# The feed-forward of a hybrid decoder layer in two phases, with seven half products for the first product too

## The chip, the cores and the metric

The kernel runs on one core of one Trainium2 chip. A core has five engines with queues of their own: TensorE (in profiles PE, its weight loads PEld), VectorE (DVE), ScalarE (ACT), GpSimd (POOL) and SyncE (SP), and 16 DMA engines that all queues share. SBUF is the working memory of 128 partitions, PSUM holds the matmul sums in banks of 512 fp32 columns. The metric is the time of one execution on the device, in microseconds (us). Given are the median of the runs and one execution recorded by the hardware profiler.

## The reference

One decoder layer for one sequence of 512 tokens, model width 2048, all in float32:

- `mod = silu(c) @ w_ada + b_ada` gives six vectors of 2048 (shift, scale and gate of the mixer, then of the feed-forward).
- `h = rmsnorm(x) * (1 + scale) + shift`, `proj = h @ w_in`, then eight HGRN2 heads and eight gated-delta heads of width 128, `y = concat(heads) @ w_out` and `x = x + gate * rmsnorm(y)`.
- The feed-forward (FF):

```python
h = rmsnorm(x, pre_ffn_norm[l]) * (1.0 + sc_f) + sh_f
y = jnp.square(jax.nn.relu(h @ w_ff1[l])) @ w_ff2[l]
x = x + gt_f * rmsnorm(y, post_ffn_norm[l])
```

`w_ff1` is 2048 x 8192, `w_ff2` 8192 x 2048. Both FF products have the same number of multiplications.

## The kernel before

**Three matmuls for one.** Every float32 matrix product is split: an operand is rounded to a high part H (`copy` into the type fp32r) and the rest is the low part L (a subtraction). `mm3` (its matmuls are recorded under line 296) multiplies H by H, H by L and L by H into one PSUM bank. So each weight piece needs a cast on ScalarE (L165) and a subtraction on VectorE (L167, for a few early pieces on GpSimd) beside its load.

**The weight stream.** `WeightStream` holds a plan of all weight pieces in the order of use. A piece is 128 partitions x 1024 floats, 512 KB. `get` hands out the split halves of the next piece and, ahead of that, issues loads on SP's queue and splits a few pieces on. SP's queue works in order: a load that waits for its buffer holds up those behind it.

**The layer's stages.** The start computes the modulation and the first projections; then the heads run while TensorE works through the remaining projections; then the output product (`pout`), in four column blocks; then the residual, the norm and 64 transposes (`pm`) that give `h2H` and `h2L`, the transposed FF input; then the FF; then norm, gate, residual and store. In the FF the order of TensorE's and SP's instructions is that of the program; the other engines' is laid out by a planner by its own costs.

**The FF before.** The 8192 inner columns are cut into 16 row blocks `r` of 512 (`RB` = 4 columns of 128). `ff1(r, g)` computes half a block (`pf`): 4 pieces, each 24 matmuls of 512 tokens; ScalarE takes Relu and Square into `g` (L1544, L1545). The second product uses Winograd's form of Strassen's scheme: both operands are cut into quarters, and seven products of sums of quarters replace eight products. `combos(r)` forms and splits the sums of activations (L1555 to L1567), `ff2s(r, m)` the seven products for half the output columns, 12 matmuls of 512 columns for each piece (`px`, `pg`). The sums of weight quarters are formed by DMAs that add to a loaded buffer, issued by GpSimd (L142, `chain`, `raw`). After each product VectorE adds the PSUM bank to the output `y2` in SBUF (L1607, L1609). The order is `ff1` of block r+1 and `ff2s` of block r in turn:

```python
for r in range(NR - 1):
    last = r == NR - 2
    yield from ((1, r + 1, 0), (2, r, 0))
    yield from ((2, r, 1), (1, r + 1, 1)) if last else ((1, r + 1, 1), (2, r, 1))
```

The last block's second product is done plainly (`plan_f2`, `ff2`). During the FF `ada_gtf` also works off the last part of `w_ada`, the FF gate: 64 loads of 256 KB, for each a product on ScalarE (L414) and a sum on GpSimd (L416), one step for every fourth weight piece; the eight `pgf` matmuls and the gate's weighting follow in the tail.

Of the kernel before, what the change touches and what calls it, by code (L numbers as in the profile page):

```python
# [8 lines left out]
F32 = mybir.dt.float32  # L9
# [48 lines left out]
ADA_REST = (4, 3, 2, 5)  # L58


def by_tiles(name, a):
# [26 lines left out]
    if name == "w_ff1":  # L88
        return a[0].reshape(4, 4, P, DFF // 256, 256).transpose(3, 0, 2, 1, 4).reshape(-1, P, 1024)
# [4 lines left out]

class WeightStream:


# [10 lines left out]
    def start(self):  # L108

        self.loads, self.upto = [], []  # L110
        for i, e in enumerate(self.plan):
            two = e[0][0] == "s2"
            if e[1] is not None:
                self.loads.append((i, e[1], e[2] if two else None))
            self.upto.append(len(self.loads))
        self.nraw = self.nw = 0
        self.wide = None

    def _raw(self, chain):
        if chain:  # L120
            return self.wide.tile([P, 1024], F32, tag="chain", name=f"chain{self.nl}", bufs=2)
        i = self.nraw
        self.nraw += 1
        pool, tag, nb = self.pool, "raw", self.bufs[0]
        if self.wide is not None and i % 2:
            pool, tag = self.wide, "raw2"
        return pool.tile([P, 1024], F32, tag=tag, name=f"raw{i}", bufs=nb)

    def _load(self):
        key, ap, kind = self.loads[self.nl]  # L130
        raw = self._raw(kind is not None and kind[0])
        self.nc.sync.dma_start(out=raw, in_=ap[0])
        if kind is not None and kind[1] is not None:
            self._add(raw, kind[1])
# [5 lines left out]
    def _add(self, raw, ap):  # L140

        self.nc.gpsimd.dma_start(out=raw, in_=ap[0], accum_op=ALU.add)  # L142

    def _split(self):
        i = self.ns
        e = self.plan[i]
        pool, nb = self.pool, self.bufs
        two = e[0][0] == "s2"
        raw = self.raw.pop(i)
        hn = ln = None  # L150
        if not two and len(e) > 2:
# [5 lines left out]
        if hn is None:  # L157
            tags = ("wh", "wl")
            if self.wide is not None and (two or len(e) == 2):
# [8 lines left out]
        if two and e[3] is not None:  # L168
            self._add(raw, e[3][1])
            self.raw[i + e[3][0]] = raw  # L170
        k = 2 if two else e[1][1]
# [4 lines left out]
        self.ns += 1  # L176

    def get(self, key):
# [3 lines left out]
        sa = self.sa if self.wide is None else 2  # L182
        su = min(n, i + 1 + max(2, sa))
        st = min(n, i + 1 + sa)
# [1600 lines left out]
```

## Time and profile before

| | |
|---|---|
| median of 3 runs | 2586.01 us (2584.15 to 2588.4) |
| the profiled execution's own time | 2584.08 us |
| its span, first to last instruction | 2582.4 us |
| mean granted TensorE clock | 0.985 |
| first FF matmul, last of the seven-product FF | 1247 us, 2501 us |
| read from HBM, written | 418.65 MB, 8.40 MB |

A row of a group reads: line, engine, operation, output <- inputs by the program's names, shape, count, then busy time in us, mean ns of one, and idle time of the engine before it with what ended it. A row of a stretch reads: start:end, length, busy time of PE, PEld, DVE, ACT and POOL with counts, granted clock, share of the DMA engines, GB/s. A row of the timeline reads: start, length, engine, line, operation. Matmuls are pipelined: the length of one is its latency, and the distance between two starts is what it costs.

### The profile page before, as it was taken

How to read it: one execution, taken by the hardware profiler on the slowest of the kernel's cores; microseconds unless marked ns; L12 is line 12 of the kernel's file. 1: busy time of each engine (PE TensorE's matmuls, PEld its weight loads, DVE VectorE, ACT ScalarE, POOL GpSimd, SP SyncE). 2: the span in 40 equal slices, each digit the busy share in tenths (PEclk: the TensorE clock that was granted, in tenths of full speed). 3: DMA queues.
4: the chain of work that ended last, by engine and by line, in shares of the span. 5: the costliest groups of instructions: out<-in, count | busy, mean ns of one | idle time of the engine just before them, and what ended most of it. 6: DMA issues, size and time to landing. Idle time of an engine off the chain costs nothing.

```text
span 2582.4 us, 34387 instructions
## 1 busy us (share of the span) xinstructions
PE 2470.5 (96%) x12627; PEld 2007.1 (78%) x12627; DVE 1733.7 (67%) x2697; ACT 1121.9 (43%) x1795; POOL 695.1 (27%) x616
## 2 busy tenths in 40 slices
PE   5889999998999899999999999999999999999998
PEld 3667777777777778788788888888888888888886
DVE  7997887768586765634657575665656666575676
ACT  5454544544444442433534444444444444444333
POOL 5561244445445440000112112212121111100003
PEclk9899999999999999999999999999999999999999
DMA  8762334444444432344466666766667666665663
GB/s 315 254 203 77 129 121 142 140 152 137 159 146 158 142 117 82 125 145 152 173 166 178 182 197 168 207 176 179 176 194 199 179 182 177 189 178 149 185 165 155
DMA packets 148903, 429.32 MB, mean 166 GB/s; under 512 B 16647, under 2 KB 21113, under 8 KB 147581
## 3 DMA queue, kind: packets, MB, share of 16 engines
q1 hardware_dynamic: 131258, 364.14, 40.5%
q0 software_dynamic: 17280, 62.92, 14.1%
q8 instruction: 99, 1.62, 0.3%
q14 instruction: 70, 0.57, 0.1%
q10 hardware_dynamic: 196, 0.06, 0.0%
HBM read 418.65 MB, written 8.40 MB: 165 GB/s over the span
## 4 chain that ended last, share of the span: by engine, by line
PE 68%; DVE 4%; POOL 1%; ACT 1%; issue 1%; DMA 1%; DVEq 0%; SPq 0%; ACTq 0%; POOLq 0%
PE pf L296 27%; PE px L296 13%; PE pg L296 10%; PE pj L296 9%; PE pout L296 7%; DVE wl L167 1%; PE pa L296 1%; DMA ada<-in_w_ada_dram 1%; POOL y L1709 0%; DVE uc L999 0%; POOL aacc L416 0%; DVE utmp L997 0%; DVE x2r L1727 0%; PE p L296 0%; DVE zkT L458 0%
## 5 line engine op out<-in xcount | busy, mean ns | idle before, releaser
L165 ACT CAST wh<-raw 128x1024 fp32r<-128x1024 f32 x422 | 443.7, 1052 | 779.8 <-PE pf L296 229.5
L167 DVE TENSOR_TENSOR wl<-raw,wh 128x1024 fp32r<-128x1024 f32 x416 | 529.2, 1276 | 365.9 <-ACT wh L165 361.8
L296 PE MATMUL pf<-h2L,wh 128*128 128x512 f32 x1024 | 399.4, 390 | 0.0
L296 PE MATMUL pf<-h2H,wh 128*128 128x512 f32 x1024 | 399.3, 390 | 0.0
L296 PE MATMUL pf<-h2H,wl 128*128 128x512 f32 x1024 | 399.1, 390 | 0.0
L416 POOL TENSOR_TENSOR aacc<-ada,aacc 128x512 f32<-128x512 f32 x180 | 268.9, 1494 | 253.5 <-ACT ada L414 242.2
L296 PE MATMUL pj<-hH,wh 128*128 128x512 f32 x768 | 324.8, 423 | 0.0
L296 PE MATMUL pj<-hH,wl 128*128 128x512 f32 x768 | 304.7, 397 | 4.4 <-DVE wl L167 4.4
L296 PE MATMUL pj<-hL,wh 128*128 128x512 f32 x768 | 303.6, 395 | 0.0
L296 PEld LDWEIGHTS pf<-h2H,wh 128*128 128x128 f32 x1024 | 192.6, 188 | 39.8
L296 PEld LDWEIGHTS pf<-h2L,wh 128*128 128x128 f32 x1024 | 192.5, 188 | 39.8
L296 PEld LDWEIGHTS pf<-h2H,wl 128*128 128x128 f32 x1024 | 192.5, 188 | 39.7
L142 POOL DMA_DIRECT2D chain<-in_w_ff_dram x90 | 79.0, 877 | 535.4 <-DVE wl L167 316.6
L167 DVE TENSOR_TENSOR wl<-chain,wh 128x1024 fp32r<-128x1024 f32 x90 | 110.9, 1233 | 160.1 <-ACT wh L165 160.1
L296 PE MATMUL px<-wh,cH 128*128 128x512 f32 x480 | 186.9, 389 | 0.4 <-DVE y L1607 0.4
L296 PE MATMUL px<-wh,cL 128*128 128x512 f32 x480 | 186.7, 389 | 0.0
L296 PE MATMUL px<-wl,cH 128*128 128x512 f32 x480 | 186.7, 389 | 0.0
L165 ACT CAST wh<-chain 128x1024 fp32r<-128x1024 f32 x90 | 94.9, 1054 | 201.9 <-PE pf L296 98.3
L296 PEld LDWEIGHTS pj<-hH,wl 128*128 128x128 f32 x768 | 146.3, 190 | 39.5 <-DVE wl L167 6.5
L296 PEld LDWEIGHTS pj<-hH,wh 128*128 128x128 f32 x768 | 146.7, 191 | 28.9
L414 ACT ACTIVATE ada<-ada,c 128x512 f32<-128x512 f32 x244 | 166.2, 716 | 0.0
L296 PEld LDWEIGHTS pj<-hL,wh 128*128 128x128 f32 x768 | 146.9, 191 | 23.4
(450 smaller groups left out, 4493.1 us busy)
## 6 DMA issues: line engine op xcount, KB each, us to landing
raw<-in_w_ff_dram SPq DMA_DIRECT2D x256, 512.0 KB, 5.0
raw<-in_w_in_dram SPq DMA_DIRECT2D x128, 512.0 KB, 3.3
ada<-in_w_ada_dram SPq DMA_DIRECT2D x256, 256.0 KB, 3.0
chain<-in_w_ff_dram POOLq DMA_DIRECT2D x90, 512.0 KB, 5.6
adas<-in_w_ada_dram SPq DMA_DIRECT2D x128, 256.0 KB, 4.3
raw<-in_w_out_dram SPq DMA_DIRECT2D x40, 512.0 KB, 3.5
chain<-in_w_ff_dram SPq DMA_DIRECT2D x30, 512.0 KB, 5.2
raw<-in_w_ff_dram POOLq DMA_DIRECT2D x30, 512.0 KB, 5.4
```

Source lines behind the costliest of these rows:

```text
L142: self.nc.gpsimd.dma_start(out=raw, in_=ap[0], accum_op=ALU.add)
L165: self.cast = self.nc.scalar.copy(out=h, in_=raw).ins
L167: eng.tensor_tensor(out=lo, in0=raw, in1=h.bitcast(F32), op=ALU.subtract)
L296: nc.tensor.matmul(ps, lhsT=lhsT, rhs=rhs, start=start, stop=stop, skip_group_check=chain)
L414: nc.scalar.activation(out=dst[:, s], in_=a[:, s], func=AF.Copy, scale=c2[:, r0 + r : r0 + r + 1])
L416: nc.gpsimd.tensor_tensor(out=acc, in0=a, in1=acc, op=ALU.add)
```

## The change

The FF is done in two phases: all first products, then all second products.

- **Phase 1.** Row block 0 is computed plainly (`ff1_plain`, 192 matmuls of 512 tokens). For blocks 1 to 15 `ff1` computes seven products: the tokens are cut into two halves of 256, the inner width of 2048 and the block's columns in two each, so each product has 2 column groups x 8 x 3 matmuls of 256 tokens. `h_sums` forms and splits the sums of `h` once; the quarter sums of the weights are formed as the second product's are. ScalarE copies partial PSUM sums out, VectorE adds them, then Relu and Square follow. `g_sums` forms the sums of the activations and `spill` writes seven 256 KB tiles of a block to DRAM.
- **Phase 2.** `ff2s(c, m)` takes two row blocks at once (the first chunk one), so a PSUM bank collects both before VectorE adds it to `y2`. `combos` reads the activation sums back from DRAM and splits them. The order of the products is 1, 2, 5, 6, 3, 7, 4; products 1, 6, 7, 4 go on in one bank, 5 and 3 in another.
- **Weight sums.** `steps_of` plans each sum of quarters: two by accumulating DMA, one on GpSimd, one on VectorE in phase 1 (`WAYS1`); two by DMA, two on GpSimd in phase 2 (`WAYS2`). Raw buffers are 3 + 7 instead of 3 + 3 and 2 for the chains, and a load is issued as soon as its buffer is free by the program's count.
- **The FF gate.** `ada_gtf` moves into the output product, three steps for each weight piece; its `pgf` matmuls come before the last two `pre_norm`s, and the finished row goes to DRAM (`gfd`) and is read back in the tail.
- In the norm before the FF the values of `h` are kept in fp32 (`hs`) for the sums; each transposed tile takes an activation and a cast on ScalarE and one subtraction.

```diff
+WAYS1 = ("dma", "pool", "dve", "dma")
+WAYS2 = ("dma", "pool", "pool", "dma")
...
+ORDER = (1, 2, 5, 6, 3, 7, 4)
+def steps_of(key, n, k, quarter, ways):
+    out = []
+    for i in ORDER:
+        for t in range(n):
+            c, d, e = ((key, q, t) for q in ("11", "22", "12"))
+            src = lambda j, q: quarter(q, t) if ways[j] == "dma" else (key, q, t)
+            loads, raw, then = {
+                1: ([(c, "11")], c, [(0, c, "12")]),
+                2: ([((key, "21", t), "21")], (key, "21", t), []),
+                5: ([(d, "22")], c, [(1, c, "22")]),
+                6: ([(e, "12")], c, [(3, c, "21"), (2, e, "22")]),
+                3: ([], d, []),
+                7: ([], e, []),
+                4: ([], c, []),
+            }[i]
...
+    PATTERN = "2212212212"
...
+        if step:
+            for how, out, src in e[4]:
+                self.uses[out] -= 1
+                o = self.raw[out]
+                if how == "dma":
+                    self.nc.gpsimd.dma_start(out=o, in_=src, accum_op=ALU.add)
+                else:
+                    self.uses[src] -= 1
+                    eng = self.nc.gpsimd if how == "pool" else self.nc.vector
+                    eng.tensor_tensor(out=o, in0=o, in1=self.raw[src], op=ALU.add)
...
+    CHUNKS = [(0,)] + [(r, r + 1) for r in range(1, NR - 1, 2)]
+    for r in range(1, NR):
+        plan += steps_of(("f1", r), 2, 8, f1_quarter(r), WAYS1)
+    for c_, rs in enumerate(CHUNKS):
+        for m in range(2):
+            plan += steps_of(("s2", c_, m), len(rs), 2, f2_quarter(rs, m), WAYS2)
...
-    ws = WeightStream(nc, wpool, plan, 3, 1, (3, 2, 2))
+    ws = WeightStream(nc, wpool, plan, 3, 1, (3, 2, 2, 7))
...
+        def on_get():
+            for _ in range(3):
+                next(gsteps, None)
...
+        def ff1(r, A):
+            G = gslots(r)
+            xs = [xbank(f"px{r}_{u}") for u in range(2)]
+            ys, es = [None] * 2, [stage(f"e{r}_{u}", (P, 4, 256)) for u in range(2)]
+            for i in ORDER:
+                for u in range(2):
+                    wH, wL = ws.get(("f1", r, i, u))
...
+                    for k in range(8):
+                        mm3(ps, wH[:, k, :], wL[:, k, :], A[i][0][:, k, :], A[i][1][:, k, :],
+                            k == 0 and i in (1, 2, 5), k == 7 and i in (2, 3, 4), i != 2)
+                    e = es[u]
+                    if i in (1, 5, 6):
+                        nc.scalar.copy(out=e[:, (1, 5, 6).index(i), :], in_=ps)
+                    elif i == 4:
+                        nc.scalar.activation(out=G[:, 0, u, :], in_=ps, func=AF.Relu)
+                    else:
...
+                        nc.vector.tensor_tensor(out=G[:, slot, u, :], in0=ps, in1=e[:, n, :], op=ALU.add)
...
+                if i == 5:
+                    spill(r - 1)
...
+        def ff2s(c, m):
...
+                for t in range(n):
+                    wH, wL = ws.get(("s2", c, m, i, t))
+                    b = cs_[(c, i)]
+                    for tb in range(2):
+                        ts = slice(tb * P, (tb + 1) * P)
+                        for jj in range(2):
+                            mm3(pss_[tb], b[:, 0, 2 * t + jj, ts], b[:, 1, 2 * t + jj, ts], wH[:, jj, :], wL[:, jj, :],
+                                i in (1, 2, 5) and t + jj == 0, i in (2, 3, 4) and t == n - 1 and jj == 1, i != 2)
+                        if t < n - 1:
+                            continue
...
+                        elif plus:
+                            nc.vector.tensor_tensor(out=dst, in0=ps, in1=dst, op=ALU.add)
...
+            A = ff1_plain()
+            for r in range(1, NR):
+                ff1(r, A)
+            for c_ in range(len(CHUNKS)):
+                for m in range(2):
+                    if m == 0 and c_ + 1 < len(CHUNKS):
+                        todo.append(combos(c_ + 1))
...
+                    ff2s(c_, m)
...
-            ps = pj(f"pgf{cb}")
-            total_of(ps, gacc2[:, cs], gf2[:, cb % 2, :], gf2[:, 2 + cb % 2, :])
-            nc.vector.tensor_tensor(out=Gf[:, cs], in0=ps, in1=Gf[:, cs], op=ALU.mult)
+        Gf = fp.tile([P, D], F32, tag="x61", bufs=1, name="Gf")
+        nc.sync.dma_start(out=Gf, in_=gfd[0].partition_broadcast(P))
```

More of the change, by code (lines that the diff above doesn't have):

```diff
@@ L92, in by_tiles @@
     return a
+ORDER = (1, 2, 5, 6, 3, 7, 4)
[14 more added lines that the diff above has]
+            }[i]
+            out.append((key + (i, t), ("step", k), [(w, quarter(q, t)) for w, q in loads], raw,
+                        [(ways[j], o, src(j, q)) for j, o, q in then]))
+    return out
 class WeightStream:
+    PATTERN = "2212212212"
     def __init__(self, nc, pool, plan, load_ahead, split_ahead, bufs):
@@ L138, in _load @@
             self.on_load(1.46)
-    def _add(self, raw, ap):
-        self.nc.gpsimd.dma_start(out=raw, in_=ap[0], accum_op=ALU.add)
     def _split(self):
         i = self.ns
+        while self.nl < self.upto[i]:
+            self._load()
         e = self.plan[i]
         pool, nb = self.pool, self.bufs
[L148 to L151, printed above, removed]
+        step = e[1][0] == "step"
+        key = e[3] if step else i
+        raw = self.raw[key]
+        self.uses[key] -= 1
+        hn = None
+        if not step and len(e) > 2:
             if isinstance(self.alt, list):
@@ L158, in _split @@
             tags = ("wh", "wl")
-            if self.wide is not None and (two or len(e) == 2):
+            if self.wide is not None and (step or len(e) == 2):
                 if self.nw % 3 == 1:
@@ L167, in _split @@
         eng.tensor_tensor(out=lo, in0=raw, in1=h.bitcast(F32), op=ALU.subtract)
[L168 to L171, printed above, removed]
+        k = e[1][1]
         self.hl[i] = (
@@ L1409, in hybrid_layer_kernel @@
     x2d = dram.tile([T, D], F32, name="x2d")
+    gfd = dram.tile([1, D], F32, name="gfd")
+    gd = [dram.tile([7 if r < NR - 1 else 4, P, T], F32, name=f"gd{r}") for r in range(NR)]
     with ExitStack() as st:
@@ L1417, in hybrid_layer_kernel, with ada_gtf @@
         junk = mp.tile([P, 1024], BF16, name="junkm")
-        R = mp.tile([P, T], F32, name="R")
+        gacc2 = mp.tile([P, D], F32, name="gacc2")
+        def ada_gtf():
+            nc.gpsimd.memset(gacc2, 0.0)
+            nc.sync.dma_start(out=gacc2[0:1, :], in_=b_ada[:, 5 * D : 6 * D])
+            queue = []
+            for i in range(4 * KT + LOOK):
+                if i < 4 * KT:
+                    cb, r = divmod(i, KT)
+                    queue.append(ada_load(lambda n: ada_pool_.tile([P, T], F32, tag="ada", bufs=LOOK + 1, name=n),
+                                          5, cb, r))
+                if i >= LOOK:
+                    cb, r = divmod(i - LOOK, KT)
+                    ada_pool(queue.pop(0), 512, r, 1, gacc2[:, cb * 512 : (cb + 1) * 512], False, ws.cast)
+                yield
+        gsteps = ada_gtf()
+        def on_get():
+            for _ in range(3):
+                next(gsteps, None)
+        ws.on_get = on_get
         def scaled(ps, tok, nb):
```

503 lines of the change are left out of this document (276 added, 227 removed).

## The prediction

> **What bounds the kernel now.** I read the share of busy time first, then the chain of waits, then stretches of the feed-forward (FF) part.
>
> ```profile
> span 2582.4 us, 34387 instructions
> PE 2470.5 (96%) x12627; PEld 2007.1 (78%) x12627; DVE 1733.7 (67%) x2697; ACT 1121.9 (43%) x1795; POOL 695.1 (27%) x616
> ```
>
> The chain of waits in order of time (start, length, what):
>
> ```profile
> 1380.52 21.76 PE pf L296 x96
> 1421.32 21.76 PE pf L296 x96
> ```
>
> ```profile
> 1320.50:2501.50 1181.00, 1180.62 (x5208) 977.13 (x5207) 752.12 (x936) 494.80 (x583) 204.75 (x180) 1.00 0.67 183
> ```
>
> The last row is one stretch: its length, then busy time of PE, PEld, DVE, ACT and POOL, granted clock, share of the DMA engines, GB/s. TensorE is busy for 1180.62 of 1181.00 us at clock 1.00, so the FF is bound by TensorE, with no gaps to win. A block of 96 matmuls of 512 columns takes 21.76 us, so one takes 21.76/96 = 0.2267 us (the 390 ns of the groups below is latency; matmuls overlap). A round of a first and a second product repeats every 1421.32 - 1380.52 = 40.80 us = 180 x 0.2267. Only fewer or shorter matmuls help, and only if the other engines keep the pace.
>
> **The matmuls.** Groups by line, with count, busy time and mean ns:
>
> ```profile
> L296 PE MATMUL pf<-h2H,wh 128*128 128x512 f32 x1024 | 399.3, 390 | 0.0
> L296 PE MATMUL px<-wh,cH 128*128 128x512 f32 x480 | 186.9, 389 | 0.4 <-DVE y L1607 0.4
> L296 PE MATMUL pg<-wh,cH 128*128 128x512 f32 x360 | 140.0, 389 | 0.0
> ```
>
> Each row stands for one of three equal groups: the first FF product (pf) has 3072 matmuls, the second (px, pg) 2520. The second keeps its count. The first keeps 4 columns x 16 blocks x 3 = 192 matmuls of 512 for row block 0; the other 15 blocks become 7 products x 2 x 8 x 3 = 336 matmuls of 256 columns each, 5040 in all. Removed: 2880 x 0.2267 = 652.8 us.
>
> What 256 columns cost, with a weight load before each, is shown by only one place, the X2 pair of the solve (matmuls first, weight loads second):
>
> ```profile
> 976.20 0.39 PE L296 MATMUL pb<-X1L,blk16r 128*128 128x512 f32 x1
> 976.44 0.28 PE L296 MATMUL pb<-X2H,blk16r 128*128 128x256 f32 x1
> 976.56 0.28 PE L296 MATMUL pb<-X2L,blk16r 128*128 128x256 f32 x1
> 976.67 0.40 PE L296 MATMUL pj<-hH,wh 128*128 128x512 f32 x1
> ```
>
> ```profile
> 976.44 0.19 PEld L296 LDWEIGHTS pb<-X2L,blk16r 128*128 128x128 f32 x1
> 976.56 0.19 PEld L296 LDWEIGHTS pj<-hH,wh 128*128 128x128 f32 x1
> ```
>
> Start to start is 0.12 and 0.11 us: (976.67 - 976.44)/2 = 0.115. The matmul starts 0.12 us after its own load began, although the load is listed with 0.19. With the other pair (rows under 252 us below) the mean is (0.115 + 0.12)/2 = 0.118. Bounds: half of 0.2267 is 0.113, a gain of 652.8 - 571.2 = 81.6 us; 0.12 gives 48.0 us. I take 0.118: 5040 x 0.118 = 594.7, **a gain of 58.1 us**, not the 81.6 that counting columns gives.
>
> ```profile
> 252.13 0.28 PE L296 MATMUL pb<-X2H,blk16r 128*128 128x256 f32 x1
> 252.25 0.28 PE L296 MATMUL pb<-X2L,blk16r 128*128 128x256 f32 x1
> 252.37 0.40 PE L296 MATMUL pph<-hH,wh 128*128 128x512 f32 x1
> ```
>
> The Trainium skill (TensorE: Matmul & The Clock Gate, Back-to-back issue gap) gives N/2.4 + 2.5 ns when warm, 109 ns for 256 columns; by that the gain would be 103 us (an estimate from that page). The trace does not agree: the same formula gives 216 ns for 512 columns where the chain shows 226.7.
>
> **The work around the matmuls.** A weight piece (512 KB) now serves 24 matmuls of 256, 24 x 0.118 = 2.83 us, in phase 1 and 12 of 512, 2.72 us, in phase 2. Before, first-product pieces lasted 5.44 us. The rows for what each piece needs:
>
> ```profile
> L165 ACT CAST wh<-raw 128x1024 fp32r<-128x1024 f32 x250 | 263.7, 1055 | 450.1 <-PE pf L296 229.5 <-PE px L296 114.3 <-PE pg L296 88.7
> L167 DVE TENSOR_TENSOR wl<-chain,wh 128x1024 fp32r<-128x1024 f32 x90 | 110.9, 1233 | 160.1 <-ACT wh L165 160.1
> L1607 DVE TENSOR_TENSOR y<-px,y 128x512 f32<-128x512 f32 x112 | 73.9, 684 | 0.7
> L1545 ACT ACTIVATE g<-g 128x512 f32<-128x512 f32 x64 | 40.4, 632 | 1.8
> L1555 DVE TENSOR_TENSOR gS<-g 128x256 f32<-128x256 f32 x60 | 24.0, 420 | 56.0 <-ACT g L1545 56.0
> L167 POOL TENSOR_TENSOR wl<-raw,wh 128x1024 fp32r<-128x1024 f32 x6 | 15.4, 2562 | 15.2 <-ACT wh L165 15.2
> L142 POOL DMA_DIRECT2D chain<-in_w_ff_dram x90 | 79.0, 877 | 535.4 <-DVE wl L167 316.6
> raw<-in_w_ff_dram SPq DMA_DIRECT2D x256, 512.0 KB, 5.0
> chain<-in_w_ff_dram POOLq DMA_DIRECT2D x90, 512.0 KB, 5.6
> ```
>
> *Phase 1*, one row block, 14 pieces, 39.6 us of TensorE: VectorE 14 x 1.23 + 2 piece sums x 1.23 + 6 sums of 256 columns x 0.42 + 4 activation sums x 0.68 = 24.9 us (63%); ScalarE 14 x 1.055 plus about 8 of copies, Relu and Square (0.63 each when 512 wide) = 23; GpSimd 2 x 2.56 + 4 x 0.88 = 8.6. *Phase 2*, one half of a chunk (14 pieces, 38.1 us): VectorE 14 x 1.23 + 14 additions x 0.68 + 3.5 splits of activations x 1.23 = 31.0 us (81%); ScalarE 18.5; GpSimd 4 x 2.56 + 4 x 0.88 = 13.8.
>
> DMA: the two queues give a price per MB.
>
> ```profile
> q1 hardware_dynamic: 131258, 364.14, 40.5%
> q0 software_dynamic: 17280, 62.92, 14.1%
> ```
>
> That is 0.405 x 2582/364 = 2.87 us of all engines per MB and 5.8 for an accumulating one. A row block moves 4 MB of weights, 2 MB accumulating and 1.8 MB of activations written: 28 us of 39.6. A half chunk moves 4 + 2 accumulating + 1.75 MB read back: 28 of 38.1. That is 0.72 to 0.74 where the stretch above has 0.67. Nothing exceeds TensorE on average; what is left is lateness in chains.
>
> *The chain of quarter sums.* One buffer c is split (cast and subtraction, 2.3 us), added to by DMA (5.6 + 0.9 to issue), split, added to on GpSimd (2.56), split, added to by DMA, split. With two blocks per product (n = 2) the first leg has 4 pieces, 10.9 us, for 8.8; the GpSimd leg 2 pieces, 5.4 us, for 4.9 plus signals; splits run two pieces (about 3 us) ahead. It just holds; I charge 0.5 us per row block for lateness (15 x 0.5 = 7; from 0 to 3 each). In the chunk with one block (n = 1) the legs are half as long: a pass takes four splits, two DMA sums and a GpSimd sum, 4 x 2.3 + 2 x 6.5 + 2.6 = 25, against 19.0 for 7 pieces; twice, less the lead of about 4: **+8** (0 to 15).
>
> *The shared accumulator.* In phase 2 product 4 follows product 7 in the same bank; it may start 1.36 us (6 matmuls) after 7 ends, and an addition of 0.68 must come between, behind a subtraction of up to 1.23. Before, another product lay between. About 0.35 us for 14 half chunks: **+5** (0 to 14).
>
> *GpSimd sums against VectorE.* This is the unknown that matters. Where both read SBUF, the rows show (GpSimd, then VectorE):
>
> ```profile
> 189.61 2.57 POOL L167 TENSOR_TENSOR wl<-raw,wh 128x1024 fp32r<-128x1024 f32 x1
> ```
>
> ```profile
> 186.19 2.31 DVE L167 TENSOR_TENSOR wl<-raw,wh 128x1024 fp32r<-128x1024 f32 x1
> 189.86 2.88 DVE L828 SCALAR_TENSOR_TENSOR hL<-ht,shm,hH 128x512 fp32r<-128x512 f32 x1
> 1526.72 1.41 DVE L1607 TENSOR_TENSOR y<-px,y 128x512 f32<-128x512 f32 x2
> 1539.41 2.30 DVE L167 TENSOR_TENSOR wl<-raw,wh 128x1024 fp32r<-128x1024 f32 x1 [0.30 <-ACT wh L165]
> ```
>
> A 1.23 us subtraction took 2.3 under a GpSimd operation, and a 512-wide one 2.88; an addition from PSUM (1526.72, two of them) stayed near 0.7. So a half chunk's 10.2 us of GpSimd sums can push back subtractions but not additions. Unblocked VectorE needs 31.0 plus some 1.5 of hand-offs of 38.1; half of the 10.2 on top gives 37.6, which still fits. I charge 1 us each: 14 x 1 = **+14** (0 to 65). The Trainium skill (SBUF — State Buffer, Who interferes with whom) says that a VectorE instruction with two SBUF inputs and a GpSimd instruction that reads SBUF exclude each other for the whole instruction, whoever starts first. The trace agrees (2.88 beside 2.57); it is the rule that speaks against this change.
>
> **What is moved.** The last adaLN part (64 loads of 256 KB, each with a ScalarE product and a GpSimd sum) goes from the FF, where it cost TensorE nothing, to the output product, three per weight piece.
>
> ```profile
> 1100.00:1155.00 55.00, 55.00 (x243) 45.31 (x242) 19.90 (x19) 17.26 (x24) 0.00 (x0) 1.00 0.43 148
> L414 ACT ACTIVATE ada<-ada,c 128x512 f32<-128x512 f32 x64 | 46.1, 720 | 0.0
> L416 POOL TENSOR_TENSOR aacc<-ada,aacc 128x512 f32<-128x512 f32 x180 | 268.9, 1494 | 253.5 <-ACT ada L414 242.2 <-PE p L296 3.9
> ```
>
> In the first 16 pieces (54 us) 48 steps need ScalarE 17 + 34.6 = 52 us, GpSimd 72 us and DMA 0.43 x 54 + 12 MB x 2.87 = 58 us. SP's queue is in order, so weight loads stand behind adaLN loads that wait for GpSimd. Against the 18 us too much stand 7 adaLN buffers (10 us) and three weight pieces (10 us): **+3** (0 to 18). The gate sums enter the gap between output and FF, where VectorE is busy already (below), with 8 operations of 0.68: +2. The sums of the activations for product 5 to 7 run on VectorE and GpSimd under the first 43 us of the FF: +2 (0 to 8). Out of the tail go eight matmuls for the gate, 8 x 0.23: -2.
>
> ```profile
> 1245.00:1258.00 13.00, 11.74 (x56) 9.93 (x56) 10.96 (x15) 6.54 (x10) 2.56 (x2) 0.70 0.03 11
> 2531.40 0.25 PE pgf L296
> ```
>
> **The sum**, against the profiled execution's 2584.08 us (span 2582.4 and 1.7 around it): -58.1 + 7 + 8 + 5 + 14 + 3 + 2 + 2 - 2 = -19.1, so 2565.0. The median of the runs, 2586.01, lies 1.9 above the profiled execution; with that the forecast is **2567 us**, and 2545 to 2590 as this case's own range.
>
> **The rivals.**
>
> *All of it hides.* Splits run ahead, DMA is at 0.74. For it: today's second product has two 0.68 us additions and a subtraction in each 2.72 us piece, over 90% of VectorE, and the chain of waits has no gap there. Against it: that lasts seven pieces and then rests during a first product; phase 2 rests nowhere. Time: 2586.0 - 58.1 + 8 - 2 = 2534.
>
> *VectorE and GpSimd become the bound of phase 2 (slower).* If subtractions wait for most of each GpSimd sum, a half chunk takes 31.0 + 1.5 + 10.2 = 42.7 instead of 38.1, 14 x 4.6 = 65 in place of 14: 2567 + 51 = 2618. It decides from 38.1 - 32.5 = 5.6 us lost per half chunk, 1.4 per sum. For it: 2.31 and 2.88 above. Against it: additions from PSUM can fill the time, and the GpSimd sum itself often waits instead (1.49 us a 512-wide sum on the mean).
>
> *The output product starves.* The 18 us of GpSimd excess come through in full, and the gap before the FF grows by 10: 2567 + 15 + 8 = 2590. Against it: the stretch 1100 to 1155 has ScalarE, VectorE and GpSimd two thirds idle or more.
>
> *Short matmuls don't get shorter.* If a steady stream goes by the weight load's listed 0.19 us, 5040 x 0.19 = 958 instead of 595: 2930. The X2 pairs speak against it, but they are only two matmuls long.
>
> *The page's gap holds in a long stream.* At 0.109 us, 5040 x 0.109 = 549, 45 less: 2522. The first matmul row above speaks against it.
>
> **How the numbers follow.** Chances: forecast 0.50, all hidden 0.17, VectorE and GpSimd bound 0.24, output starves 0.05, not shorter 0.02, shorter still 0.02. About 0.2% (5 us) is what a measurement of this kernel can tell from no change. The forecast's own range gives 0.44 faster and 0.06 the same; hidden and shorter still are faster; of the 0.24, light forms are 0.01 faster and 0.04 the same, 0.19 slower; of starving, 0.02 the same. Together 0.64 faster, 0.12 the same, 0.24 slower. The range reaches down past the hidden case to 2525, and up to 2625, past the slower case; beyond lie the last two rivals and the ends of several terms at once.
>
> **What would show it.** Starts of first-product matmuls 0.118 us apart and about 39.6 us for a row block (right), 0.113 or 0.19 (wrong). In phase 2 38.1 us per half chunk if hidden, 39 to 40 as forecast, 42 or more with TensorE waiting on VectorE's subtractions or additions if the slower rival holds; subtractions of 2.3 us and longer in number beside GpSimd's sums. In the chunk with n = 1 a pass of 22 to 25 us instead of 19. In the output product an unbroken stretch of TensorE, as now, but for a few us. The prediction is wrong if TensorE's waits in the two phases add up to less than 10 or more than 70 us, or if a wait for a DMA load (not a sum) leads them.

## The result and the profile after

The changed kernel is **slower**: 2627.74 us (median of 4 runs, 2625.23 to 2630.04) against 2585.08 us for the kernel before beside it. The ratio is 1.0163, with a 95% interval of 1.0145 to 1.018. The forecast was 2567 us with a range up to 2625 us, so sign and range both missed. The profiled execution took 2626.21 us, its span 2624.5 us: 42.1 us longer than before.

The share of busy time, and the DMA queues (packets, MB, share of 16 engines), of the changed kernel:

```profile
span 2624.5 us, 39183 instructions
PE 2448.3 (93%) x14787; PEld 2072.3 (79%) x14787; DVE 1876.3 (71%) x2610; ACT 1256.9 (48%) x1998; POOL 951.5 (36%) x714
...
q1 hardware_dynamic: 157388, 406.62, 45.3%
q0 software_dynamic: 17280, 62.92, 13.4%
```

TensorE has less work than before but is now busy for 93% of the span instead of 96%. Where it waits is seen by stage (columns as before: start:end, length, then busy PE, PEld, DVE, ACT, POOL, granted clock, DMA share, GB/s). The rows are the output product, the gap and row block 0, phase 1, the chunk with n = 1, the 14 half chunks, and the tail:

```profile
1053.40:1249.20 195.80, 185.36 (x823) 148.22 (x820) 98.91 (x117) 109.44 (x172) 108.78 (x73) 1.00 0.68 229
1249.20:1321.60 72.40, 60.39 (x272) 48.30 (x271) 63.07 (x79) 42.40 (x70) 26.68 (x18) 0.88 0.40 132
...
1321.60:1926.40 604.80, 604.80 (x5041) 604.76 (x5041) 397.39 (x395) 320.36 (x442) 129.08 (x91) 1.00 0.73 205
1926.40:1983.70 57.30, 42.73 (x171) 32.71 (x170) 37.31 (x34) 29.38 (x38) 14.73 (x9) 0.94 0.76 215
1983.70:2567.10 583.40, 549.22 (x2354) 440.73 (x2353) 456.47 (x439) 248.34 (x245) 200.05 (x108) 0.99 0.68 196
2567.10:2624.50 57.40, 43.65 (x193) 35.82 (x191) 32.79 (x43) 16.52 (x37) 22.04 (x17) 0.92 0.19 74
```

Phase 1 is one unbroken stream of 604.8 us. Phase 2 is not: before, such a stretch had TensorE busy for 1180.62 of 1181.00 us; here 34 us are plain gaps, and the busy time itself holds the latency of matmuls ahead of gaps. The ledger sets these lengths against the kernel before. Its first- and second-product stages are interleaved, so they are counted as matmuls by 0.2267 us; "forecast" is the prediction's own term for that stage.

| stage (us) | before | after | difference | forecast |
|---|---|---|---|---|
| output product | 183.3 | 195.8 | +12.5 | +3 |
| gap and row block 0 | 62.1 | 72.5 | +10.4 | +4 |
| row blocks 1 to 15 of the first product | 652.8 | 604.8 | -48.0 | -58.1 + 7 |
| second product, chunk with n = 1 | 38.1 | 57.2 | +19.1 | +8 |
| second product, 14 half chunks | 533.1 | 583.4 | +50.3 | +5 + 14 |
| tail | 58.9 | 57.4 | -1.5 | -2 |

The differences add up to +43, against 42.1 measured (the rest is small gaps in the FF before, which the count leaves out). So the gain came, 48 of the 51 us forecast for those rows, and four other stages gave back 92.3.

**Phase 1** in the timeline, TensorE's matmuls and then its weight loads:

```profile
1599.80 0.28 PE L328 MATMUL px<-hA,wl 128*128 128x256 f32 x1
1599.92 0.28 PE L328 MATMUL px<-hA,wh 128*128 128x256 f32 x1
1600.04 0.28 PE L328 MATMUL px<-hB,wh 128*128 128x256 f32 x1
```

```profile
1599.92 0.19 PEld L328 LDWEIGHTS px<-hB,wh 128*128 128x128 f32 x1
1600.04 0.19 PEld L328 LDWEIGHTS px<-hA,wl 128*128 128x128 f32 x1
```

Starts are 0.120 us apart, here and over the stage: 604.8/5040 = 0.120. Nothing else shows in it.

**Phase 2** has three kinds of rows that stand out beside the kernel before. The first are the waits of ScalarE in the 14 half chunks (total, times, longest), below its usual wait for TensorE to free a weight buffer:

```profile
ACT wh L202 <- PE qx L328: 144.3, 79, 5.4
ACT wh L202 <- POOL raw L220: 59.6, 23, 3.9
...
ACT c L1732 <- DMA cs<-gd: 23.9, 8, 6.0
ACT hA L1732 <- DMA cs<-gd: 21.8, 7, 5.8
ACT hB L1732 <- DMA cs<-gd: 16.9, 8, 4.7
```

The groups of VectorE's weight subtractions and GpSimd's weight sums in the same stretch:

```profile
L204 DVE TENSOR_TENSOR wl<-raw,wh 128x1024 fp32r<-128x1024 f32 x196 | 286.5, 1465 | 96.6 <-ACT wh L202 95.6 <-DMA cs<-gd 0.7
L220 POOL TENSOR_TENSOR raw<-raw,raw 128x1024 f32<-128x1024 f32 x54 | 153.7, 2854 | 310.8 <-DVE wl L204 142.0 <-DMA raw<-in_w_ff_dram 140.2 <-DVE Y L1816 28.5
```

And one half chunk in the timeline, ScalarE, VectorE, GpSimd, TensorE in turn (start, length, then in brackets the idle time before and its releaser):

```profile
2158.30 1.05 ACT L1732 CAST c<-cs 128x1024 fp32r<-128x1024 f32 x1 [6.05 <-DMA cs<-gd]
2159.26 1.03 ACT L202 CAST wh<-raw 128x1024 fp32r<-128x1024 f32 x1
...
2160.53 1.22 DVE L204 TENSOR_TENSOR wl<-raw,wh 128x1024 fp32r<-128x1024 f32 x1
2162.80 3.41 DVE L204 TENSOR_TENSOR wl<-raw,wh 128x1024 fp32r<-128x1024 f32 x1
...
2161.83 3.29 POOL L220 TENSOR_TENSOR raw<-raw,raw 128x1024 f32<-128x1024 f32 x1 [11.04 <-DVE wl L204]
...
2160.34 0.50 PE L328 MATMUL qy<-wh,c 128*128 128x512 f32 x1 [1.03 <-ACT wh L202]
2161.80 0.50 PE L328 MATMUL qy<-wl,c 128*128 128x512 f32 x1 [0.95 <-DVE wl L204]
2166.26 0.50 PE L328 MATMUL qy<-wl,c 128*128 128x512 f32 x1 [1.41 <-DVE wl L204]
```

The reader sees a chain. ScalarE comes to the cast of an activation sum (L1732) whose read-back is still in flight, and waits 6.05 us. The weight cast due next stands behind it and follows at once, without a wait of its own. TensorE runs out of split weights (1.03). The split whose end releases the GpSimd sum is late too, so the sum starts after 11.04 us of idleness, just when VectorE catches up on subtractions. One of these then takes 3.41 us instead of 1.22 (1.41 more for TensorE).

The load is late because it is issued late. The chain of waits at the same place (start, length, what):

```profile
2151.87 0.32 SPq L1755
...
2152.23 5.99 DMA cs<-gd
...
2158.30 1.06 ACT c L1732
```

There are two staging buffers for the read-back (tag `st`), so SP issues the load (L1755) when an earlier activation split is done, at 2151.87, and the landing takes 5.99 us.

The planner, by its own costs, placed each activation cast in ScalarE's order. From the profile alone three causes could bear the 50 us: the read-back, the GpSimd sums, and the order of the casts. The experiments take them one by one.

### The profile page after: what moved, and what is told of

The parts are those of the page before. It is cut to its first block, busy times and chain, and to the rows that moved or that the text cites. A ratio compares the mean times of both kernels' runs of the same rounds, so it can differ in the third digit from the quotient of the medians.

```text
span 2624.5 us, 39183 instructions
## 1 busy us (share of the span) xinstructions
PE 2448.3 (93%) x14787; PEld 2072.3 (79%) x14787; DVE 1876.3 (71%) x2610; ACT 1256.9 (48%) x1998; POOL 951.5 (36%) x714
## 4 chain that ended last, share of the span: by engine, by line
PE 50%; DVE 11%; DMA 6%; issue 4%; POOL 3%; ACT 3%; SPq 0%; DVEq 0%; POOLq 0%; ACTq 0%
PE px L328 13%; PE pj L328 9%; PE py L328 7%; PE qx L328 5%; PE pout L328 5%; DVE wl L204 4%; PE pz L328 4%; DMA raw<-in_w_ff_dram 3%; PE qy L328 3%; DMA cs<-gd 2%; ACT wh L202 1%; POOL gacc L448 1%; POOL raw L220 1%; DMA ada<-in_w_ada_dram 1%; PE pf L328 1%
## 5 line engine op out<-in xcount | busy, mean ns | idle before, releaser
L204 DVE TENSOR_TENSOR wl<-raw,wh 128x1024 fp32r<-128x1024 f32 x595 | 838.6, 1411 | 409.6 <-ACT wh L202 406.1
L202 ACT CAST wh<-raw 128x1024 fp32r<-128x1024 f32 x601 | 628.1, 1049 | 864.5 <-PE pj L328 169.4
L220 POOL TENSOR_TENSOR raw<-raw,raw 128x1024 f32<-128x1024 f32 x90 | 241.5, 2689 | 480.8 <-DVE wl L204 290.3
L448 POOL TENSOR_TENSOR aacc<-ada,aacc 128x512 f32<-128x512 f32 x180 | 269.2, 1496 | 253.4 <-ACT ada L446 242.1
L216 POOL DMA_DIRECT2D raw<-in_w_ff_dram x120 | 105.5, 879 | 401.3 <-DVE wl L204 397.5
L328 PEld LDWEIGHTS pj<-hH,wl 128*128 128x128 f32 x768 | 146.3, 190 | 39.4 <-DVE wl L204 6.4
L328 PE MATMUL qx<-wh,c 128*128 128x512 f32 x480 | 154.8, 393 | 3.4 <-ACT wh L202 3.4
L328 PE MATMUL px<-hA,wl 128*128 128x256 f32 x480 | 135.8, 283 | 0.0
L328 PE MATMUL px<-hB,wh 128*128 128x256 f32 x480 | 135.8, 283 | 0.0
L328 PE MATMUL px<-hA,wh 128*128 128x256 f32 x480 | 135.8, 283 | 0.0
L328 PE MATMUL qx<-wl,c 128*128 128x512 f32 x240 | 95.8, 399 | 13.7 <-DVE wl L204 13.7
L437 DVE SCALAR_TENSOR_TENSOR asum<-adas,c,asum 128x256 f32<-128x256 f32 (+1 forms) x150 | 105.3, 713 | 2.4
L328 PE MATMUL pout<-wh,oH 128*128 128x512 f32 x256 | 101.8, 399 | 5.3 <-ACT wh L202 3.5
```

The costliest lines, as they stand in the source:

```text
L202: self.cast = self.nc.scalar.copy(out=h, in_=raw).ins
L204: eng.tensor_tensor(out=lo, in0=raw, in1=h.bitcast(F32), op=ALU.subtract)
L216: self.nc.gpsimd.dma_start(out=o, in_=src, accum_op=ALU.add)
L220: eng.tensor_tensor(out=o, in0=o, in1=self.raw[src], op=ALU.add)
L328: nc.tensor.matmul(ps, lhsT=lhsT, rhs=rhs, start=start, stop=stop, skip_group_check=chain)
L437: nc.vector.scalar_tensor_tensor(out=acc, in0=av, scalar=cv, in1=acc, op0=ALU.mult, op1=ALU.add)
```

## The experiments

Stage times of every kernel, from first to last matmul starts (us; the half chunk is the mean of 14). Without any stall a half chunk is 168 matmuls, 38.1.

| kernel | time | output | gap, block 0 | n = 1 | half chunk | last half |
|---|---|---|---|---|---|---|
| the change | 2626.21 | 195.8 | 72.5 | 57.2 | 41.66 | 44.0 |
| a1_nopool | 2584.24 | 196.5 | 71.9 | 40.5 | 39.83 | 43.1 |
| a2_noread | 2605.59 | 195.2 | 72.6 | 57.1 | 40.23 | 45.5 |
| a3_neither | 2575.01 | 195.5 | 73.3 | 41.3 | 38.97 | 42.3 |
| a4_pace_behind | 2589.07 | 187.4 | 74.4 | 55.3 | 39.40 | 44.3 |
| b1_c0 | 2580.15 | 188.7 | 75.1 | 44.6 | 39.43 | 44.0 |
| b2_own4 | 2604.49 | 187.5 | 76.5 | 48.8 | 40.79 | 44.5 |
| b3_gate_tail | 2590.97 | 188.7 | 73.1 | 56.4 | 39.37 | 45.0 |
| b4_behind_nopool | 2579.05 | 187.3 | 76.8 | 50.8 | 39.04 | 43.1 |
| c1_all | 2586.03 | 191.5 | 80.2 | 44.1 | 39.37 | 41.4 |
| c2_nohlate | 2582.15 | 191.6 | 79.3 | 44.7 | 39.06 | 38.5 |
| d1_best | 2571.99 | 187.6 | 76.6 | 44.6 | 39.01 | 38.5 |
| d2_nohsums | 2562.27 | 188.8 | 64.5 | 44.7 | 39.11 | 38.5 |

Times of c1, c2 and d1 are medians of repeated runs, the others one execution each; the kernel before took 2584.7 to 2586.0 beside them. Phase 1 stays at 604.8 to 606.7 in all.

### Sums and read-back, each taken away and both

**a1_nopool** leaves out GpSimd's weight sums in phase 2, and in the chunk with n = 1 all sums:

```
     for how, out, src in e[4]:
+        if e[0][0] == "s2" and (how == "pool" or e[0][1] == 0):
+            if how != "dma":
+                self.uses[src] -= 1
+            continue
```

> Left out: in phase 2 the quarter sums on GpSimd, and in the first chunk (one row block) all quarter sums, those by DMA too. Changed kernel now: 41.7 us per half chunk (14 of them, 38.1 of matmuls), first chunk 57.2 us (38.1 of matmuls). Theory 1, GpSimd's sums hold up VectorE's subtractions and the pieces that wait for them: half chunks of 38.5 to 39.5 us, 30 us or more off the time. Theory 2, the read-back of the activation sums is late and stands at the head of ScalarE's queue: half chunks stay at 40.5 or more. For the first chunk: 38 to 41 us if its chain of sums sets its time, 50 or more if the spill and the reads at the phase border do.

**a2_noread** leaves out the loads of the read-back from the third chunk on; the splits run on what is in the staging buffers:

```
-    raws[i] = stage(f"cs{c}_{i}", (P, 4, 256))
-    for d, r in enumerate(CHUNKS[c]):
+    if c >= 2:
+        raws[i] = KEEP[n % 2]
+    else:
+        raws[i] = stage(f"cs{c}_{i}", (P, 4, 256))
+        KEEP[n % 2] = raws[i]
+    for d, r in enumerate(CHUNKS[c] if c < 2 else ()):
```

> Left out: the loads that read the activation sums back from DRAM for the third and later chunks; the splits of activations run on what lies in the two staging buffers. Theory 1 (GpSimd's sums against VectorE): half chunks from the third chunk on stay at 40.5 us or more. Theory 2 (ScalarE waits for the read-back, with weight casts behind it): 38.5 to 39.5 us, about 25 us off the time. If both take a share: 39.5 to 40.5.

**a3_neither** does both.

> Left out: both of the above. If the two causes are all, half chunks come to 38.1 us of matmuls plus the hand-off between products 7 and 4 in one bank, 0.5 to 0.7 us: 38.6 to 38.8. More than 39.5 means that a third cause is left (VectorE's own load, DMA loads of weights).

Without the sums a half chunk is 1.83 us shorter, without the read-back 1.43, without both 2.69: 14 x 2.69 = 37.7 of the 50.3 us. In a3 every half chunk but the last takes 38.70 to 38.73. The two single effects add up to 3.26, more than both together, so they lean on one another: each is enough to make the weights late, and taking away one leaves the other. (These are single executions; the difference, 14 x 0.57 = 8 us, is more than the 4.8 us between the change's shortest and longest run.) Neither theory alone, sums or read-back, is right. In the chunk with n = 1, a1 takes 40.5 instead of 57.2, so there the sums are the cause. a2 leaves the loads of that chunk as they are, and it takes 57.1.

### The order of ScalarE alone

**a4_pace_behind** leaves all work in. It puts each activation cast behind the newest weight cast in ScalarE's order, and (apart from that) takes two adaLN steps instead of three for each of the first 16 weight pieces of the output product:

```
     def on_get():
-        for _ in range(3):
+        ngets.append(0)
+        for _ in range(2 if len(ngets) <= 16 else 3):
...
     def c_split(c, i, raw):
-        nc.scalar.copy(out=b[:, 0], in_=raw)
+        with tc.issue_after(ws.cast):
+            nc.scalar.copy(out=b[:, 0], in_=raw)
```

> Nothing left out. Two edits: in the first 16 pieces of the output product two adaLN steps for each piece instead of three; and the cast of the activation sums stands in ScalarE's queue behind the newest weight cast. Output product: 12.5 us longer than before now; if GpSimd's rate (1.5 us a sum) holds the weight loads up, 0 to 4 us longer; if it is DMA bandwidth, 8 or more. Phase 2: theory 2 expects half chunks of 39 to 40.5 us, theory 1 no change from 41.7.

A half chunk falls from 41.66 to 39.40, 14 x 2.26 = 31.6 us, with every sum and every load still there (the pace of adaLN ends 700 us earlier); 7 of the 14 take 38.70 to 38.73, as in a3. The ScalarE waits in the 14 half chunks:

```profile
ACT wh L202 <- PE qx L328: 156.1, 101, 2.9
ACT wh L202 <- POOL raw L220: 45.6, 23, 2.5
...
ACT wh L202 <- DMA cs<-gd: 5.0, 3, 1.7
```

The 62.6 us in which activation casts waited for the read-back are gone from the list, and 5.0 us remain; ScalarE's longest single wait for TensorE to free a weight buffer falls from 5.4 to 2.9 us, and such waits are more frequent (101 instead of 79 on `qx`), which is what running ahead steadily looks like. And the groups, VectorE and GpSimd, of the same stretch:

```profile
L204 DVE TENSOR_TENSOR wl<-raw,wh 128x1024 fp32r<-128x1024 f32 x196 | 291.7, 1496 | 82.2 <-ACT wh L202 78.8 <-DMA cs<-gd 2.5
L220 POOL TENSOR_TENSOR raw<-raw,raw 128x1024 f32<-128x1024 f32 x54 | 139.0, 2578 | 303.8 <-DMA raw<-in_w_ff_dram 181.6 <-DVE wl L204 92.0 <-DVE Y L1819 29.7
```

The subtractions are **as long as before the repair** (1496 ns on the mean, 1465 in the change). So the lengthening of VectorE's work, which the slower rival charged, is there in both kernels, and only one of them pays much for it. In phase 1 of the change the same subtractions take 1381 ns on the mean, and TensorE has no gap there. GpSimd's waiting has moved from the split (142.0 to 92.0) to the landing of its load (140.2 to 181.6): the splits now come earlier.

**b4_behind_nopool** is a4 without GpSimd's sums in phase 2 (the lines of a1 with `how == "pool"` alone).

> Built on run a4. Left out: the quarter sums on GpSimd in phase 2 (a1's edit, with the first chunk's DMA sums kept). In a4 the half chunks from the third chunk on take 39.0 us without the last; 38.7 is matmuls and hand-off. Theory: with ScalarE's order mended VectorE and GpSimd have slack enough, so that leaving the sums out gains 0.5 us a half chunk at most. If the lock of the two is a bound by itself, long subtractions (2.3 us and more) should be what is left in a4, and this run falls to 38.7 in every half chunk while a4's irregular ones (39.4 to 40.6) vanish.

Its subtractions are back at their short length:

```profile
L204 DVE TENSOR_TENSOR wl<-raw,wh 128x1024 fp32r<-128x1024 f32 x196 | 239.8, 1223 | 140.5 <-ACT wh L202 140.5
```

52 us of VectorE's time less (291.7 - 239.8) shorten the 14 half chunks by 0.36 us each, 5 us in all. With the order mended, then, the sums cost 5 us; in the change, taking them away is worth 25.6. The sign that the expectation gave for a lock of the two engines is there in small: 13 of b4's 14 half chunks take 38.71 to 38.82, and a4's irregular ones (up to 40.6) are gone.

### What is left in phase 2

**b2_own4** (a4, and product 4 in a bank of its own, which costs two more VectorE additions per half chunk):

```
-                if i in (1, 6, 7, 4):
+                if i in (1, 6, 7):
...
-                elif i == 2:
+                elif i in (2, 4):
...
+                        elif i == 7:
+                            nc.vector.tensor_tensor(out=k21, in0=ps, in1=k21, op=ALU.add)
```

> Built on run a4; nothing left out. Edit: product 4 opens a bank of its own (product 2's) instead of going on in the bank that product 7 has just filled; two more additions a half chunk on VectorE. The hand-off theory expects the 0.62 us that every half chunk has over its 38.08 us of matmuls to go: 38.1 in the undisturbed ones. If VectorE is at its limit, the two additions (1.4 us) cost more than that: 39.5 or more.

The waits of TensorE in the half chunks of the change (first), and of b2 (second):

```profile
PE qy L328 <- DVE wl L204: 12.1, 12, 1.5
PE qx L328 <- DVE wl L204: 10.5, 12, 1.2
PE qx L328 <- DVE Y L1816: 7.3, 14, 1.9
```

```profile
PE qx L328 <- DVE wl L204: 13.2, 21, 1.9
PE qy L328 <- DVE wl L204: 4.4, 7, 0.8
```

The hand-off from product 7 to product 4 (L1816, 14 times, 0.52 us each; 38.7 - 38.1 = 0.6 with what the restart costs) is gone in b2, but a half chunk is 1.39 us longer than in a4. VectorE is the reason that its row gives:

```profile
1974.20:2545.20 571.00, 549.90 (x2353) 441.29 (x2352) 494.78 (x474) 249.80 (x245) 197.42 (x112) 0.99 0.70 203
```

It is busy for 494.78 of 571.00 us, 87%, and TensorE's waits for subtractions are back: 13.2 and 4.4 us, where a4 has 2.4 and 0.2. So VectorE is close to a bound of phase 2, and the shared bank is worth more than its wait.

**b1_c0** (a4, and in the chunk with n = 1 the sums on GpSimd and VectorE in turn instead of by DMA):

```
+    one = n == 1
+    if one:
+        ways = ("pool", "dve", "pool", "dve")
...
-                1: ([(c, "11")], c, [(0, c, "12")]),
+                1: ([(c, "11")] + [(e, "12")] * one, c, [(0, c, "12")]),
...
-                6: ([(e, "12")], c, [(3, c, "21"), (2, e, "22")]),
+                6: ([(e, "12")] * (not one), c, [(3, c, "21"), (2, e, "22")]),
```

> Built on the kernel of run a4 (two adaLN steps, activation cast behind the weight cast); nothing left out. Edit: in the chunk with one row block no sum goes by DMA: the first on GpSimd, the second and the last on VectorE, e on GpSimd, from buffers loaded for it. If the chain of sums sets that chunk's 55.3 us (two passes, 38.1 of matmuls), a pass needs 4 splits of 2.3 plus 2.7 + 1.2 + 1.2, 14 us, and the chunk comes to 40 to 44. If VectorE's load sets it (about 19.5 of 19.0 us a pass with these sums): 46 to 50. If the phase border does (spill, read-back): above 52.

The chunk takes 44.6 instead of 55.3, just above the 40 to 44 expected of a chain of sums. In the change, the chain of waits of that chunk is led by loads, the accumulating ones among them (its summary by line):

```profile
by line: DMA raw<-in_w_ff_dram 47.1%; DVE wl L204 16.0%; issue 15.4%; PE qx L328 8.2%; ACT wh L202 5.8%; POOL raw L220 4.3%; DVE Y L1816 2.7%; DVE hB L1733 2.0%; ACT c L1732 1.7%; DVE Y L1814 1.2%; ACT Y L1812 1.1%; ACTq L202 0.1%; DVE c L1
```

The row does not part plain loads from adding ones; the runs do. Of the change's 19.1 us, 16.7 go when there are no sums (a1, 40.5). Of a4's 17.2, 10.7 go when the same sums are made by engines: these 10.7 belong to the DMA sums.

TensorE's longest wait in that chunk of the change is another one:

```profile
PE qx L328 <- DVE Y L1816: 8.3, 2, 6.0
```

It is the hand-off from product 7 to product 4, once in each pass, 2.3 and 6.0 us; in the second pass the subtraction from PSUM stands on VectorE behind a weight subtraction of 3.24 us. The prediction charged this hand-off in the 14 half chunks alone. b2, which opens a bank for product 4 and keeps the DMA sums, takes 48.8 here against a4's 55.3. So the sums make the chunk late, and the hand-off makes it later; the two shares overlap and are not parted further.

**b3_gate_tail** (a4, and the gate's `pgf` matmuls and weighting back in the last half chunk and the tail, with the sums of adaLN through DRAM, and the residual's loads issued after the first half of the plain product):

```
-        total_of(ps, gacc2[:, cs], gsplit[:, 0, :], gsplit[:, 1, :])
...
-    nc.sync.dma_start(out=gfd, in_=gacc2[0:1, :])
+    nc.sync.dma_start(out=gfd, in_=gacc2)
...
+    mm(ps, onesr, gaH[:, cs], True, False)
+    mm(ps, onesr, gaL[:, cs], False, True)
```

> Built on run a4; nothing left out. Two edits in stages apart. (1) The FF gate's column sums leave the gap between output product and FF; the accumulator goes to DRAM and is finished in the last half chunk. From the last output matmul to the end of row block 0: 74.4 us in a4, 61.9 before the change (192 matmuls). If the gate's VectorE work in the gap costs its length: 68 to 70; if the sums of the activations and the later start of matmuls between the transposes do: 73 or more. (2) The residual's loads (4 MB) are issued after the last plain pieces' loads. If they starve those loads, the last half chunk falls from 44.3 to 39.5 to 41; if not, it stays.

The gap is 1.3 us shorter and the tail 1.6 longer: the gate isn't what made the gap long. The last half chunk stays at 45.0, so the residual's loads aren't its cause either.

### The last half chunk, the pace of adaLN, and the sums of h

In a4 the last half chunk still took 44.3 us. ScalarE's timeline there:

```profile
2515.19 1.04 ACT L202 CAST hA<-raw 128x1024 fp32r<-128x1024 f32 x1 [6.80 <-DMA raw<-in_w_ff_dram]
2516.14 1.99 ACT L202 CAST wh<-raw 128x1024 fp32r<-128x1024 f32 x2
```

It is the same defect at another place: the cast of a piece for the plain part (block 15), not due until later, waits 6.80 us for its load, and two weight casts stand behind it.

**c1_all** is b1 with three more edits: plain pieces' casts behind the newest weight cast, one and two adaLN steps per piece in turn, and the sums of `h` formed after a later column of row block 0:

```
-        self.cast = self.nc.scalar.copy(out=h, in_=raw).ins
+        if hn and self.tc is not None and self.wide is not None:
+            with self.tc.issue_after(self.cast):
+                self.cast = self.nc.scalar.copy(out=h, in_=raw).ins
+        else:
+            self.cast = self.nc.scalar.copy(out=h, in_=raw).ins
...
+        for _ in range(1 + len(ngets) % 2 if len(ngets) <= 16 else 3):
...
-                if a == 0:
-                    out = h_sums()
...
+                    if (a, j) == (1, 0):
+                        out = h_sums()
```

> Built on run b1; nothing left out. Three more edits, each in a stage of its own: (1) adaLN steps one and two in turn for the first 16 pieces of the output product; (2) the casts of the plain pieces at the end stand behind the weight casts before them on ScalarE; (3) the sums of the activations for the seven products are formed after the fifth plain piece of row block 0 instead of the fourth. Expected by stage: output product 188.7 to 184 to 187; last half chunk 44 to 39 to 41 if ScalarE's order is its cause, unchanged if the loads themselves are late; from the last output matmul to the first seven-product matmul 75 to 70 to 73 if VectorE's work there is what delays the plain pieces, or a new wait at row block 1 if the sums come too late for product 5. Time: 2567 to 2576, 0.4 to 0.7% below the kernel before.

**c2_nohlate** is c1 with the sums of `h` where the change has them.

> As run c1, but without its third edit: the stage between output product and row block 1 stays at 75 us. Time: 2570 to 2575, ratio to the kernel before 0.995 to 0.998. If c1 is slower than this one, the later sums cost more at product 5 than they free before.

c1 took 2586.03 us (ratio to before 1.0008, 0.9998 to 1.0018), c2 2582.15 (0.9991, 0.9981 to 1.0), both longer than expected. The last half chunk falls to 38.5 in c2 (41.4 in c1; no run explains the rest). Two of the edits missed. Later sums did not shorten the gap (80.2 against 79.3). And the slower pace, by which alone c2 differs from the next kernel, d1, lengthened the output product (191.6 against 187.6) and the gap (79.3 against 76.6). The traces show a likely reason, which no run tests by itself. With fewer adaLN steps on the first pieces more are left for the last: in c2 GpSimd's sums hold 11.8% of the output product's chain of waits, against 1.8% in d1, and from 1219 to 1232 us it runs through these sums to a step of the norm that stands behind them on GpSimd.

**d1_best** is therefore b1 with the plain pieces' casts behind the weight casts, and the pace of a4.

> Built on run b1 with the second edit of c1 alone (casts of the plain pieces behind the weight casts), so with two adaLN steps for each of the first 16 pieces; nothing left out. By stage: output product 187 to 189, then 74 to 77 to row block 1, row blocks 604.8, first chunk 44.6, half chunks 39.1 on the mean with the last one under 40. Time: 2573 to 2578, ratio to the kernel before 0.995 to 0.998. If pacing one and two in turn was no loss, it equals run c2 instead (0.999).

Its last half chunk takes 38.5, where b1, without the order of the plain pieces, has 44.0: that order was the cause. The kernel takes **2571.99 us** (median of 5 runs, 2571.47 to 2576.81) beside 2585.65 for the kernel before: ratio 0.9953, interval 0.9939 to 0.9966. Its stretches, the output product, the gap and block 0, phase 1, the chunk with n = 1 and the half chunks:

```profile
1052.10:1239.70 187.60, 183.16 (x821) 148.66 (x820) 95.87 (x115) 104.21 (x167) 108.86 (x72) 1.00 0.72 235
1239.70:1316.20 76.50, 61.77 (x272) 49.88 (x271) 64.48 (x82) 45.01 (x75) 26.91 (x18) 0.89 0.41 135
1316.20:1920.90 604.70, 604.70 (x5040) 604.66 (x5040) 394.07 (x392) 320.19 (x442) 126.04 (x90) 1.00 0.74 205
1921.00:1965.60 44.60, 40.63 (x170) 32.37 (x169) 43.69 (x40) 29.78 (x39) 10.83 (x5) 0.96 0.60 204
1965.60:2511.80 546.20, 538.68 (x2352) 439.62 (x2352) 465.68 (x439) 248.21 (x243) 186.78 (x111) 1.00 0.74 212
```

It does all the work of the change; VectorE is even busier in the half chunks (465.68 against 456.47 us), and they take 37.2 us less.

**d2_nohsums** is d1 without the sums of `h` and their splits (`h_sums` returns unsummed blocks, so products 3, 5, 6 and 7 have other inputs).

> Built on d1. Left out: the sums of the activations h and their splits for products 3, 5, 6 and 7 (these use unsummed blocks). From the last output matmul to row block 1: 75 us in b1, 61.9 before the change for the same matmuls. If VectorE's and GpSimd's work on these sums delays row block 0: 64 to 68. If it is the norm's own chain (two ScalarE operations a tile, the gate in the gap, no matmuls between the transposes): 71 or more.

The gap and row block 0 (compare with the second row above):

```profile
1241.40:1306.00 64.60, 58.02 (x273) 46.67 (x272) 41.66 (x57) 34.56 (x58) 10.64 (x10) 0.95 0.45 154
```

It is 12 us shorter, and VectorE has 22.8 us less to do in it (64.48 - 41.66). In d1 VectorE is busy for 84% of this stretch. In the change TensorE's longest wait of this stage is for a weight split on VectorE:

```profile
PE pf L328 <- DVE wl L204: 6.5, 1, 6.5
```

So the sums of `h` with their splits cost 12 us in d1, not the 2 (at most 8) of the prediction.

## Why the prediction was wrong

**The matmul of 256 columns: right in kind, one term off.** The prediction took 0.118 us from two pairs in the solve, with 0.12 as the upper bound. A stream of 5040 takes 0.120 each, so the gain is 48.0 instead of 58.1. The bound from the row held; both rivals that had other prices (0.19 and 0.109) fell. The formula that the Trainium skill (TensorE: Matmul & The Clock Gate, Back-to-back issue gap) gives for an isolated gap comes to 109 ns for 256 columns. The runs do not agree: 120 ns.

**Phase 1's lateness: overcharged.** Charged 7, measured 0: the stage has no gap between two of its matmuls. "It just holds" was right without the surcharge. That the two terms together (-51) came so near to the measured -48 is luck: errors of 10 and 7 us cancel.

**The half chunks: the step that failed.** 5 + 14 were charged, 50.3 came. The step is the balance of phase 2, where ScalarE's 18.5 us of 38.1 and the read-back's share of the DMA engines were taken as all there is to them. Busy time was right (ScalarE 248.34/14 = 17.7 per half), but ScalarE works in order. The planner put a cast that waits for a 6 us landing ahead of casts that TensorE needs within the next 3 us. The prediction asked what is queued behind a waiting instruction for SP, and never for ScalarE. Its last paragraph came near, with "a wait for a DMA load (not a sum)" as a sign of being wrong, but gave it no price and looked for it among TensorE's waits. There it does not lead: TensorE waits for VectorE's subtractions (12.1 and 10.5 us), the mean half chunk is 41.66 us, and the two phases lose 69 us, just under the 70 that were to show the prediction wrong. By these signs the loss looks like the slower rival; only the order of ScalarE, changed alone in phase 2 (a4), tells the two apart. a4 shows that the order alone is worth 31.6 of the 50.3 us, and d1 (546.2 for the stretch) that with the plain pieces 37.2 go; of the 13.1 that stay, the hand-off (0.6 x 14 = 8.4, charged 5) is most.

**The slower rival was nearest in time (2618), but is not the cause as it was put.** It said that subtractions pushed back by GpSimd's sums make VectorE the bound. The subtractions did get longer, by 286.5 - 196 x 1.22 = 47 us. The Trainium skill (SBUF — State Buffer, Who interferes with whom) says that a VectorE instruction with two SBUF inputs contends with a GpSimd instruction that reads SBUF, for a port pair under an exclusive lock. The trace agrees: the subtraction of 3.41 us began within a sum of 3.29 us and ended 1.09 us after it. But in a4 they are as long, and the half chunks take 39.4. The collision costs when the splits are already late, and 5 us when they are not (b4). That VectorE has little left is true (b2, 87%), so it is a limit close by, not the one reached.

**The chunk with n = 1: mechanism right, size off, one wait left out.** 25 us for a pass was forecast, less a lead of 4 for both; the passes took 24.0 and 33.3. The first is close to the forecast, the second is not. In the chain of waits of the second pass the two accumulating loads took 8.4 and 7.0 us with their issue, where 6.5 was charged, and the hand-off to product 4, not charged in this chunk, took 6.0. Replacing the chain of DMA sums by engine sums gives 44.6.

**The output product: a rival came true in small.** "The output product starves" was given 0.05. Its mechanism is what happened. The summary of the chain of waits in that stage, the change first, then d1:

```profile
by line: PE pout L328 66.4%; POOL gacc L448 14.1%; DMA ada<-in_w_ada_dram 5.8%; DMA raw<-in_w_out_dram 2.3%; DMA wpost<-in_post_mix_norm_dram 2.0%; ACT wh L202 1.6%; ACT ada L446 1.5%; DVE wl L204 1.3%; issue 1.2%; PE hpo L328 0.8%; ACT jun
```

```profile
by line: PE pout L336 68.9%; DVE wl L212 3.4%; ACT wh L210 3.2%; DMA raw<-in_w_out_dram 2.9%; DMA ada<-in_w_ada_dram 2.8%; issue 2.5%; DMA wpost<-in_post_mix_norm_dram 2.2%; DVE z L1501 2.1%; DMA raw<-in_w_ff_dram 2.1%; POOL gacc L457 1.8%;
```

GpSimd's sums of adaLN hold 14.1% of the chain in the change and 1.8% at two steps per piece. Charged 3, measured 12.5, of which 8.4 go with the pace. The failed step is the cushion: seven buffers and three pieces were to swallow 15 of 18 us of excess, and 8 to 12.5 came through.

**The gap before the FF:** charged 4, measured 10.4. The gate was rightly small (b3), the sums of `h` were not (d2): they were charged as if hidden under row block 0, in a stretch where VectorE had been quoted as busy for 10.96 of 13.00 us.

**The tail** was right (-1.5 against -2).

Added up, the errors are 10 for the matmul, -7 for phase 1, 31 for the half chunks, 11 for n = 1, 9.5 for the output product and 6.4 for the gap: half of the 62 us between -19 and +43 lies in one unasked question. With the order of ScalarE put right in two places, the chunk's sums moved and the pace lowered, the kernel gains 13.7 us on the one before.

## What to carry to other kernels

For every engine that works in order, ask what stands behind each instruction that waits for a DMA, ScalarE's casts too, and look for the row "engine line <- DMA" with a long longest wait; busy shares don't show it. When two causes each seem to explain a loss, take away each and both: single effects that add up to more than the joint one point to one chain. Work that lengthens (here VectorE's subtractions) costs little while the stream runs ahead (here 5 us, against 25.6 when it is late), so mend what makes the stream late first.

## What the runs showed of the hardware

- A matmul of 256 columns with a weight load before each starts every 0.120 us in a stream of 5040, with granted clock 1.00; the load is listed with 0.19 us and the matmul with 0.28. That is 53% of the 0.2267 us for 512 columns.
- VectorE's subtraction of 128x1024 takes 1.22 us alone and 3.41 beside a GpSimd sum of the same size, which itself takes 2.58 us on the mean (a4) to 2.85 (the change). Additions from PSUM do not show it: in the half chunks of the change their mean is that of the kernel before, 684 ns, or a little less:

```profile
L1814 DVE TENSOR_TENSOR Y<-qx,Y 128x512 f32<-128x512 f32 x55 | 35.1, 676 | 0.0
```
- A read-back of 256 KB from DRAM took 5.99 us to land in the middle of phase 2, where the stage's mean DMA share is 0.68.
